# An encoder trunk on one Trainium2 core: a pair of sums, the weight sums, the variance and conv's squares change places

## The chip, the cores and the metric

The kernel runs on one core of a Trainium2 chip. The metric is the time of one launch on the device in microseconds; of several runs the median is taken. TensorE (PE) multiplies, VectorE (DVE) and ScalarE (ACT) do the work element by element, SyncE's queue (SP) issues the transfers of weights.

## The reference

Two layers run over two sequences of 512 and 256 tokens, 768 columns in all. Layer 0 mixes tokens by windowed attention, layer 1 by a gated convolution of width 3. Each layer then has a feed-forward network and a gated embedding.

```python
D_MODEL, D_FF, DEPTH = 1024, 4096, 2
def trunk(x, p, ...):
    for i in range(DEPTH):
        h = rms_norm(x, norm_mix[i])
        x = x + (window_attention if i % 2 == 0 else short_conv)(h, ...)
        h = rms_norm(x, norm_mlp[i])
        x = x + jnp.square(jax.nn.relu(h @ mlp_w_up[i])) @ mlp_w_down[i]
        gate = jax.nn.sigmoid(rms_norm(x, norm_ple[i]) @ ple_w_gate[i])
        x = x + (p[i] @ ple_w_proj[i]) * gate
    return rms_norm(x, final_norm)

def rms_norm(x, g):
    return x * lax.rsqrt(jnp.mean(x * x, axis=-1) + EPS) * g

def short_conv(h, w_in, conv_w, w_out):
    b_gate, c_gate, u = jnp.split(h @ w_in, 3, axis=-1)
    ...   # z = c_gate * u, three taps of z, times b_gate
    return (b_gate * conv) @ w_out
```

## The kernel before

**Layout.** Features lie on the partitions, the 768 tokens on the free axis. x is eight blocks of 128 features by 768 tokens. Most matmuls are 128 by 128 by 384, half the tokens (`H`).

**Precision.** A float32 operand is split into a high part, which ScalarE makes by a copy (`whi`, `zhi`, `vhi`), and a low part, which VectorE makes by a subtraction (`wlo`, `zlo`, `vlo`, line 443). A product takes high by high, high by low and low by high. So a chunk of weights is ready only when VectorE has made its low part.

**Seven products in place of eight.** Large products are done as seven block products over sums of blocks (a scheme of Strassen's kind). Both operands need sums: of the weights `sums32` and `sums14` (lines 405 to 413, two VectorE steps of 128x512 each), of the normalised input `combine(m)` for each m of four. A `combine` pairs blocks m and m+4 of x: two ScalarE copies scaled by the gain (`q`), four VectorE steps 384 wide (`t13` and `t42`, lines 343 to 349), two ScalarE copies for the high parts and two VectorE steps 768 wide for the low parts (`t`, line 359). The first two chunks of a feed-forward's up projection, and the first chunks of conv, are done plainly instead (`up_plain`, `plain_product`, line 1474), because the sums aren't ready yet.

**Norms.** The division by the root mean square is put off: products are made from `xs`, x times the gain, and the scale `r` is applied to the results. `Norm.block` runs for each block of x when it is done: it makes high and low `xs` (line 310 and 311 for the second half of the blocks) and adds the block's squares to `acc` (line 199). The sum of squares over the partitions is a product with ones (`ss`, line 238), its parts `ah` and `al` are split on line 86 and 87. `rstd_steps` then gives five steps, `logs` (variance `v`, line 255, and a logarithm), `root`, `square`, `newton` and `result`.

**Where it happens.** Layer 0's output projection runs over the blocks in the order 0, 4, 1, 5, 2, 6, 3, 7 (`PAIRED`), i counting the places. For each it multiplies (`mm`, line 132), adds to x (`add`, line 1280), runs `n1.block`, then `behind(i)` of `second_inputs`, which loads and splits the second layer's embedding input and its projection (at i = 3) and the first weights. After it come the `pj` products of `ahead`, 48 matmuls, and then the feed-forward: two plain chunks u = 0 and 1, the first seven-product chunk u = 2, an up chunk u = 3, and from there down and up chunks in turn. In `ahead` VectorE makes the low part of the first weights, `acc`'s parts and combined pairs 0 and 1. Layer 1 has conv in the place of attention; its norms and its feed-forward work the same way.

**What sets the order.** ScalarE, TensorE and VectorE each run their instructions in the order in which the code above issues them (`manual_schedule`); no scheduler moves them. So the place of a call in the code is the place in the queue. `pend` is a list of steps that `late()` takes one at a time and issues between the steps of a chunk: in `seven_parts` they are the squares and sums of the chunk before. PSUM's eight banks are shared under the tags A, B and C.

**Names.** In `seven_parts`, `a`, `b`, `c` and `d` are PSUM banks of the products, `y` the chunk's result, `act` its high and low parts. `y L1592` is `y22`, VectorE's read of `a` and of p after the s1 product. The product with w22 uses `vhi` and `vlo`, that with s2 and s3 `zhi` and `zlo`.

## Time and profile before

| | |
|---|---|
| median of three runs | 1646.12 us (1645.8, 1646.12, 1646.88) |
| profiled execution | 1647.11 us, its span 1645.3 us |
| granted TensorE clock | 0.998 |
| busy: TensorE, its weight loads | 99%, 96% of the span |
| busy: VectorE, ScalarE, GpSimd | 84%, 56%, 1% |
| chain that ended last | PE 90%, DVE 5%, DMA 2%, ACT 2%, issue 1% |
| DMA | 144.80 MB, mean 88 GB/s, 27.8% of the 16 engines |

A row of a timeline gives the start in the span and the busy time (both us), the engine, the line, the operation, output<-input, the shape and how many alike were run together; in brackets, how long the engine had been idle before and what it had waited for. A row of the waits gives engine, buffer and line, what released it, the total wait, its count and its longest. PEld is TensorE's weight load, which runs beside the matmul ahead of it.

Where the places lie in the span: layer 0's output projection runs from about 262 to 287 us, the pj products to 295.7, the first plain chunk from 295.7, the second from 313.1, the first seven-product chunk from 329.8. Conv starts at 840.9. Layer 1's feed-forward starts at 1088.3, its first seven-product chunk at 1122.3.

### The profile page before, as it was taken

The page shows a single profiled execution, that of the slowest core. Times are in us where ns is not written, and L with a number is a line of the kernel's source. Part 1 is how long each engine was busy: PE and PEld are TensorE (multiplying, and loading weights), DVE is VectorE, ACT ScalarE, POOL GpSimd, SP SyncE. Part 2 cuts the span into 40 slices and gives each one's busy share as a digit, 9 for nine tenths or more (in the row PEclk, how much of TensorE's full clock was granted, in tenths as well). Part 3 has the DMA queues.
Part 4 walks back from the last instruction along what each step waited for, and adds up shares of the span by engine and source line. Part 5 has one row for each costly group of instructions (what it writes and reads, how often), then busy time and mean ns, then how long its engine had stood idle before and what let it go on. Part 6 is the DMA issues. An engine that isn't in the chain of part 4 may idle for free.

```text
span 1645.3 us, 24138 instructions
## 1 busy us (share of the span) xinstructions
PE 1627.5 (99%) x9371; PEld 1575.4 (96%) x9371; DVE 1389.8 (84%) x2212; ACT 920.7 (56%) x1458; POOL 12.3 (1%) x60
## 2 busy tenths in 40 slices
PE   9999999999999999999999999999999999999998
PEld 7988889999999999999999999999999999999987
DVE  7578987999899989977878888769989989999686
ACT  7378884765555545545654344555545555655465
POOL 0000000000000000000000000000000000000000
PEclk9999999999999999999999999999999999999999
DMA  8745303222221222232311222211222222222332
GB/s 309 193 131 135 107 26 96 93 75 74 68 77 66 76 65 85 70 93 78 116 61 52 77 77 77 78 52 53 76 67 85 67 68 74 78 67 75 118 97 87
DMA packets 47822, 144.80 MB, mean 88 GB/s; under 512 B 6075, under 2 KB 9531, under 8 KB 47708
## 3 DMA queue, kind: packets, MB, share of 16 engines
q1 hardware_dynamic: 47708, 143.27, 27.8%
q8 instruction: 73, 1.20, 0.3%
q14 instruction: 41, 0.34, 0.1%
HBM read 123.85 MB, written 9.96 MB: 81 GB/s over the span
## 4 chain that ended last, share of the span: by engine, by line
PE 90%; DVE 5%; DMA 2%; ACT 2%; issue 1%; SPq 0%; DVEq 0%; POOL 0%; ACTq 0%; POOLq 0%
PE a L464 32%; PE b L464 8%; PE mm L132 8%; PE mm L680 8%; PE d L464 5%; PE c L464 5%; PE p L1474 4%; PE gate L1811 4%; PE B L464 4%; PE C L464 4%; PE gate L132 2%; PE down L1811 2%; PE pt L1129 1%; PE O L1144 1%; PE S L1086 1%
## 5 line engine op out<-in xcount | busy, mean ns | idle before, releaser
L432 ACT ACTIVATE whi<-sum 128x1024 fp32r<-128x1024 f32 x66 | 70.2, 1063 | 253.4 <-PE a L464 251.7
L464 PE MATMUL a<-xs,whi 128*128 128x384 f32 x608 | 118.0, 335 | 1.3 <-DVE y L1592 1.3
L464 PEld LDWEIGHTS a<-xs,whi 128*128 128x128 f32 x608 | 106.4, 188 | 2.3 <-DVE y L1592 2.0
L464 PE MATMUL b<-t,zhi 128*128 128x384 f32 x528 | 106.7, 334 | 0.0
L464 PE MATMUL a<-t,zhi 128*128 128x384 f32 x528 | 106.6, 334 | 0.0
L464 PE MATMUL a<-t,whi 128*128 128x384 f32 x528 | 106.6, 334 | 0.0
L1633 DVE TENSOR_TENSOR x<-x,a 128x384 f32<-128x384 f32 x112 | 62.1, 554 | 51.3 <-PE a L464 51.2
L464 PE MATMUL a<-act,whi 128*128 128x384 f32 x448 | 95.6, 334 | 0.0
L464 PEld LDWEIGHTS a<-t,whi 128*128 128x128 f32 x528 | 92.9, 188 | 0.0
L464 PEld LDWEIGHTS b<-t,zhi 128*128 128x128 f32 x528 | 92.9, 188 | 0.0
L464 PEld LDWEIGHTS a<-t,zhi 128*128 128x128 f32 x528 | 92.9, 188 | 0.0
L432 ACT ACTIVATE zhi<-sum 128x1024 fp32r<-128x1024 f32 x66 | 69.8, 1058 | 38.5 <-DVE sum L408 32.7
L443 DVE TENSOR_TENSOR wlo<-wraw,whi 128x1024 fp32r<-128x1024 f32 x72 | 87.6, 1217 | 0.0
L432 ACT ACTIVATE whi<-wraw 128x1024 fp32r<-128x1024 f32 x72 | 75.7, 1051 | 19.3 <-issue 15.6
L680 PE MATMUL mm<-xs_mix,whi 128*128 128x512 f32 (+1 forms) x320 | 81.4, 341 | 0.0
L443 DVE TENSOR_TENSOR zlo<-sum,zhi 128x1024 fp32r<-128x1024 f32 x66 | 80.3, 1217 | 0.5 <-ACT zhi L432 0.5
L443 DVE TENSOR_TENSOR wlo<-sum,whi 128x1024 fp32r<-128x1024 f32 x66 | 80.4, 1218 | 0.0
L464 PEld LDWEIGHTS a<-act,whi 128*128 128x128 f32 x448 | 79.3, 188 | 0.0
L464 PE MATMUL a<-xs,wlo 128*128 128x384 f32 x304 | 64.9, 334 | 0.0
L464 PE MATMUL b<-t,zlo 128*128 128x384 f32 x264 | 61.1, 335 | 0.7 <-DVE zlo L443 0.7
L464 PE MATMUL a<-t,zlo 128*128 128x384 f32 x264 | 60.9, 334 | 0.0
L464 PE MATMUL a<-t,wlo 128*128 128x384 f32 x264 | 60.9, 334 | 0.0
(391 smaller groups left out, 4480.2 us busy)
## 6 DMA issues: line engine op xcount, KB each, us to landing
wraw<-in_up SPq DMA_DIRECT2D x64, 512.0 KB, 3.4
wraw<-in_down SPq DMA_DIRECT2D x64, 512.0 KB, 3.5
wraw<-in_w_in SPq DMA_DIRECT2D x24, 512.0 KB, 3.4
wraw<-in_gate SPq DMA_DIRECT2D x16, 512.0 KB, 3.5
wraw<-in_w_q SPq DMA_DIRECT2D x8, 512.0 KB, 6.2
wraw<-in_w_out SPq DMA_DIRECT2D x8, 512.0 KB, 3.6
x_in<-in_x SPq DMA_DIRECT2D x8, 384.0 KB, 6.9
pj<-L SPq DMA_DIRECT2D x8, 384.0 KB, 5.7
```

Of the source, the lines that this page charges most:

```text
L132: pe.matmul(t, lhsT=w, rhs=x[:, o:e], start=first and i == 0 and j == 0, stop=last and i == n - 1 and j == 2)
L432: act.activation(hi[:], src, AF.Copy)
L443: dve.tensor_tensor(lo[:], src, hi[:].bitcast(F32), ALU.subtract)
L464: pe.matmul(ps, lhsT=a, rhs=b, start=start and i == 0, stop=i == len(terms) - 1, skip_group_check=True)
L680: pe.matmul(ps.t[:, :n], lhsT=a_, rhs=b_, start=k == 0 and j == 0, stop=k == len(xs) - 1 and j == 2,)
L1086: pe.matmul(S.t[:, :w], lhsT=q, rhs=khh_[g].t[:, kk], start=True, stop=False)
L1129: pe.transpose(pt.t[:, h * P : (h + 1) * P], lg[h // 2].t[:, h % 2, 1 + b * P : 1 + (b + 1) * P], ident[:],)
L1144: pe.matmul(O.t[:], lhsT=vb, rhs=part.t[:], start=b == 0 and i == 0, stop=b == nk - 1 and i == 1)
L1474: pe.matmul(ps[i][o], lhsT=wt[:, c], rhs=xs[f"x{h + 1}{1 + o}"][m][part], start=k == 0 and j == 0, stop=k == KB - 1 and j == 2,)
L1633: dve.tensor_tensor(t[:, o : o + H], t[:, o : o + H], f, op)
L1811: pe.matmul(ps.t[:, o : o + n], lhsT=a_, rhs=b_, start=begin and i == 0 and j == 0, stop=end and i == len(terms) - 1 and j == 2,)
```

## The change

There are four edits. They add and drop no step: each one moves steps in the order in which they are issued.

1. In layer 0's feed-forward, `combine(0)` is issued in the output projection, right behind the third block (i = 2). It takes four places of its own (`apart`). `ahead` now issues pairs 1 and 2 instead of 0 and 1, and the first plain chunk pair 3 alone instead of 2 and 3.
2. In the first plain chunk, `rooted` gives way to `woven`: the variance (`logs`) and the first step of the last pair come ahead of the low part of the next weights (layer 1), and the pair's steps are spread otherwise between the root's steps.
3. In `seven_parts`, the first seven-product chunk of each feed-forward (`soon`) makes the weight sums `sums32` of the next chunk right behind the copy to `c`, ahead of the previous chunk's steps, and no longer behind the copy to `p`.
4. In conv's first plain chunk, the product of the squares with ones, and the variance steps behind it, stand after the first two of the eight blocks of the second product instead of ahead of it; the other six blocks follow.

```diff
 class Norm7:
+            self.apart = self.free if apart is None else list(apart)
 ...
         def combine(self, m):
-            sums = Sums(None, None, [self.free.pop(0) for _ in range(4)], self.xs, m)
+            sums = Sums(None, None, [self.apart.pop(0) for _ in range(4)], self.xs, m)
+    def woven(steps, combined, w):
+        if w:
+            w.high("direct")
+        run(steps, 1)
+        run(combined, 1)
+        if w:
+            w.low("direct")
+        run(combined, 2)
+        run(steps, 1)
+        run(combined, 2)
+        run(steps, 1)
+        run(combined)
+        run(steps)
 def second_inputs(norm, places): def behind(i):
+            elif i == 2:
+                run(norm.combine(0))
 def ahead:
-        c0, c1 = (norm.combine(i) for i in range(2))
+        c0, c1 = (norm.combine(i) for i in (1, 2))
 def seven_parts(w, xs, make, then, first, late, out, soon=False):
         act.activation(c, a, AF.Copy)
+        if more7 and soon:
+            v.sums32()
         late(3 if first else 1)
 ...
         act.activation(p, b, AF.Copy)
-        if more7:
+        if more7 and not soon:
             v.sums32()
 def up_plain (u == 0):
-                v, c0, c1 = w1, *(norm.combine(m) for m in todo)
+                v, *c = w1, *(norm.combine(m) for m in todo)
 ...                                                  # product is set in layer 0
                         v.split("direct")
-                        run(c0, 2)
+                        run(c[-1], 2)
                         norm.table()
                         ss = norm.sum_squares(psum, parts=parts, tag="C")
-                        run(c0)
-                        run(c1, 2)
                     else:
                         parts = norm.acc_parts()
-                        two(c0, c1)
+                        two(*c)
 ...
                             ss = norm.sum_squares(psum, parts=parts, tag="C")
-                            v.split("direct")
-                        rooted(norm.rstd_steps(psum, ss), c1)
+                        woven(norm.rstd_steps(psum, ss), c[-1], None if product else v)
 def up:
-            v = seven_parts(w, xs, make, then, u == PLAIN[l], late, out)
+            v = seven_parts(w, xs, make, then, u == PLAIN[l], late, out, u == PLAIN[l])
 mlp:
-                todo = todo[2:]
+                todo = todo[3:]
 mixer_conv: plain
             products(0, 1)
+            plain_product(ps[0], w, xs, 1, (0, 2), (0, 1))
             ss = norm.sum_squares(psum, parts=sq, tag="C")
 ...
-            for n in range(2, 4):
-                products(0, n)
+            plain_product(ps[0], w, xs, 1, (2, 6), (0, 1))
+            products(0, 3)
             products(1, 0)
 layer 0's output projection:
-    n1 = Norm7(2, "mlp0", xs0, act0[7:11], act0[11])
-    behind, product, w0 = second_inputs(xs0[24:])
+    n1 = Norm7(2, "mlp0", xs0[:12], act0[7:11], act0[11], apart=xs0[12:])
+    behind, product, w0 = second_inputs(n1, xs0[24:])
```

VectorE's instructions in the second half of layer 0's output projection, before the change. `x` behind `xa,mm` is the add of a projected block, `xs` and `x` behind `vec` the low parts of the scaled input, `acc_mlp` the sum of squares, `wlo` the low part of proj's weights:

```order
L1280 TENSOR_TENSOR x<-xa,mm 128x384 x2
L311 SCALAR_TENSOR_TENSOR xs_3313<-x,vec,xs_3312 128x768
L199 TENSOR_TENSOR acc_mlp_3236<-acc_mlp_3236,sq 128x768
L1280 TENSOR_TENSOR x<-xa,mm 128x384 x2
L87 TENSOR_TENSOR wlo<-wraw,whi 128x1024
L306 SCALAR_TENSOR_TENSOR xs_3353<-x,vec,xs_3353 128x384
L306 SCALAR_TENSOR_TENSOR x_3354<-x,vec,x_3354 128x384
```

The same place with the change; `q` are the four 384-wide steps of the pair, `t` its two low parts, one line number is added by the edit:

```order
L1281 TENSOR_TENSOR x<-xa,mm 128x384 x2
L344 TENSOR_TENSOR q<-q 128x384
L312 SCALAR_TENSOR_TENSOR xs_3313<-x,vec,xs_3312 128x768
L199 TENSOR_TENSOR acc_mlp_3236<-acc_mlp_3236,sq 128x768
L345 TENSOR_TENSOR q<-q 128x384
L1281 TENSOR_TENSOR x<-xa,mm 128x384 x2
L349 SCALAR_TENSOR_TENSOR q<-q 128x384
L360 TENSOR_TENSOR t_3369<-q,t_3368 128x768
L307 SCALAR_TENSOR_TENSOR xs_3353<-x,vec,xs_3353 128x384
L307 SCALAR_TENSOR_TENSOR x_3354<-x,vec,x_3354 128x384
L199 TENSOR_TENSOR acc_mlp_3236<-acc_mlp_3236,sq 128x768
L350 SCALAR_TENSOR_TENSOR q<-q 128x384
```

Six steps of the pair now stand between the adds of x (the last, a second `t`, is below the rows shown), and the low part of proj's weights moves behind them.

VectorE in the first seven-product chunk of layer 0's feed-forward, before. `sum` are the weight sums, `act` the parts of the chunk before, `y` behind `y` the sums of that chunk's results, `vlo` the low part for w22:

```order
L443 TENSOR_TENSOR wlo<-sum,whi 128x1024
L389 TENSOR_TENSOR act<-y_3858,act 128x384
L343 TENSOR_TENSOR y_3858<-y_3858 128x384
L344 TENSOR_TENSOR y_3858<-y_3859,y_3858 128x384
L392 TENSOR_TENSOR act<-y_3859,act 128x768
L443 TENSOR_TENSOR vlo<-wraw,vhi 128x512
L348 SCALAR_TENSOR_TENSOR y_3859<-y_3858,y_3859 128x384
L349 SCALAR_TENSOR_TENSOR y_3859<-y_3859 128x384
L407 TENSOR_TENSOR sum<-wraw 128x512
L408 TENSOR_TENSOR sum<-sum,wraw 128x512
```

The same with the change:

```order
L444 TENSOR_TENSOR wlo<-sum,whi 128x1024
L408 TENSOR_TENSOR sum<-wraw 128x512
L409 TENSOR_TENSOR sum<-sum,wraw 128x512
L390 TENSOR_TENSOR act<-y_3858,act 128x384
L344 TENSOR_TENSOR y_3858<-y_3858 128x384
L345 TENSOR_TENSOR y_3858<-y_3859,y_3858 128x384
L393 TENSOR_TENSOR act<-y_3859,act 128x768
L444 TENSOR_TENSOR vlo<-wraw,vhi 128x512
```

The two sums have moved from behind the six steps of the chunk before to ahead of them.

TensorE in conv's first plain chunk, before and then with the change; `p` are the plain products, `ss` the four matmuls with ones:

```order
L1474 MATMUL p_8801<-xs_8769,zlo 128x384
L1474 MATMUL p_8802<-xs_8769,zlo 128x384
L238 MATMUL ss<-ah,ones 128x384
L238 MATMUL ss<-al,ones 128x384
L238 MATMUL ss<-ah,ones 128x384
L238 MATMUL ss<-al,ones 128x384
L1474 MATMUL p_8803<-xs_8242,whi 128x384
```

```order
L1494 MATMUL p_8803<-xs_8313,wlo 128x384
L1494 MATMUL p_8804<-xs_8313,wlo 128x384
L238 MATMUL ss<-ah,ones 128x384
L238 MATMUL ss<-al,ones 128x384
L238 MATMUL ss<-ah,ones 128x384
L238 MATMUL ss<-al,ones 128x384
L1494 MATMUL p_8803<-xs_8400,whi 128x384
```

Twelve matmuls of the second product, p_8803 and p_8804, now stand between the first product and `ss`.

More of the change, by code (lines that the diff above doesn't have):

```diff
@@ L287, in trunk_kernel, with __init__ @@
     class Norm7(Norm):
-        def __init__(self, i, name, places, aside, acc, rstd=None):
+        def __init__(self, i, name, places, aside, acc, rstd=None, apart=None):
             super().__init__(i, name, places, acc, rstd)
             self.free, self.x12 = list(places), list(aside)
+            self.apart = self.free if apart is None else list(apart)
             self.xs = {k: {} for k in (*QS7.values(), "x12")}
@@ L1344, in trunk_kernel, with second_inputs @@
     ET = mybir.EngineType
-    def second_inputs(places):
+    def second_inputs(norm, places):
         part = [], []
@@ L1409, in ahead, with seven_parts @@
         return parts, v
-    def seven_parts(w, xs, make, then, first, late, out):
+    def seven_parts(w, xs, make, then, first, late, out, soon=False):
         w.low("s32")
```

## The prediction

> **What bounds the kernel now.** I read the page first, then the waits of TensorE and of its weight loads (PEld), then the timelines round each wait.

> ```profile
> PE 1627.5 (99%) x9371; PEld 1575.4 (96%) x9371; DVE 1389.8 (84%) x2212; ACT 920.7 (56%) x1458; POOL 12.3 (1%) x60
> ```

> TensorE has work nearly all the time. The number of matmuls does not change, so the change can only move TensorE's waits. The list of waits, matmul rows alone, has three kinds that stand where the diff edits:

> ```profile
> PE a L464 <- DVE y L1592: 1.3, 2, 1.1
> PE b L464 <- DVE zlo L443: 0.7, 2, 0.4
> PE ss L238 <- DVE al L87: 0.2, 1, 0.2
> ```

> That is 2.2 us in five waits. The weight loads tell more. They follow each other without a hole in steady work, and here are the five places, each with the row ahead and the row behind:

> ```profile
> 340.16 1.40 PEld L464 LDWEIGHTS d<-t,vhi 128*128 128x128 f32 x8
> 341.55 0.71 PEld L464 LDWEIGHTS d<-t,vlo 128*128 128x128 f32 x4
> 343.65 1.36 PEld L464 LDWEIGHTS a<-xs,whi 128*128 128x128 f32 x8 [1.40 <-DVE y L1592]
> 345.00 0.71 PEld L464 LDWEIGHTS a<-xs,wlo 128*128 128x128 f32 x4
> ...
> 347.78 0.71 PEld L464 LDWEIGHTS b<-t,zhi 128*128 128x128 f32 x4
> 349.17 0.30 PEld L464 LDWEIGHTS b<-t,zlo 128*128 128x128 f32 x2 [0.69 <-DVE zlo L443]
> 349.46 0.71 PEld L464 LDWEIGHTS b<-t,zhi 128*128 128x128 f32 x4
> ...
> 849.05 0.19 PEld L238 LDWEIGHTS ss<-ah,ones 128*128 128x128 f32 x1
> 849.80 0.19 PEld L238 LDWEIGHTS ss<-al,ones 128*128 128x128 f32 x1 [0.56 <-DVE al L87]
> 850.26 0.19 PEld L1474 LDWEIGHTS p<-xs,whi 128*128 128x128 f32 x1
> ...
> 1133.89 0.71 PEld L464 LDWEIGHTS d<-t,vlo 128*128 128x128 f32 x4
> 1135.15 1.36 PEld L464 LDWEIGHTS a<-xs,whi 128*128 128x128 f32 x8 [0.56 <-DVE y L1592]
> 1136.50 0.71 PEld L464 LDWEIGHTS a<-xs,wlo 128*128 128x128 f32 x4
> 1139.28 0.71 PEld L464 LDWEIGHTS b<-t,zhi 128*128 128x128 f32 x4
> 1140.68 0.30 PEld L464 LDWEIGHTS b<-t,zlo 128*128 128x128 f32 x2 [0.69 <-DVE zlo L443]
> 1140.97 0.19 PEld L464 LDWEIGHTS b<-t,zhi 128*128 128x128 f32 x1
> ```

> The eight loads at 340.16 take 1.39 us to the next group, 0.174 each. From 341.55 to 345.00 twelve loads should take 2.08 us and took 3.45, so the first wait costs 1.37. In the same way 347.78 to 349.46 loses 0.64 (six loads), 849.05 to 850.26 loses 0.51 (four; two rows between are not shown), 1133.89 to 1136.50 loses 0.53 and 1139.28 to 1140.97 loses 0.65. Together **3.70 us**: this is all that the change can gain. The two places at 343 and 1135 are the first seven-product chunk of each feed-forward, the two at 349 and 1140 the first down chunk behind it, 849 is conv.

> [...]

> **The change part by part.**

> *Sums of a pair during the output projection (layer 0).* The first pair's steps leave VectorE's stretch behind 296 us, where VectorE runs without rest up to 343, and enter the projection, where it rests now and then:

> ```profile
> 271.26 1.02 DVE L311 SCALAR_TENSOR_TENSOR xs<-x,vec,xs 128x768 fp32r<-128x768 f32 x1 [1.00 <-ACT xs L310]
> 272.20 0.95 DVE L199 TENSOR_TENSOR acc_mlp<-acc_mlp,sq 128x768 f32<-128x768 f32 x1
> 273.19 1.02 DVE L1280 TENSOR_TENSOR x<-xa,mm 128x384 f32<-128x384 f32 x2
> ...
> 276.35 0.95 DVE L199 TENSOR_TENSOR acc_mlp<-acc_mlp,sq 128x768 f32<-128x768 f32 x1
> 277.22 1.01 DVE L1280 TENSOR_TENSOR x<-xa,mm 128x384 f32<-128x384 f32 x2
> 279.24 1.02 DVE L311 SCALAR_TENSOR_TENSOR xs<-x,vec,xs 128x768 fp32r<-128x768 f32 x1 [1.01 <-ACT xs L310]
> ...
> 285.67 1.02 DVE L1280 TENSOR_TENSOR x<-xa,mm 128x384 f32<-128x384 f32 x2 [0.72 <-PE mm L132]
> ...
> 294.19 1.22 DVE L443 TENSOR_TENSOR zlo<-wraw,zhi 128x1024 fp32r<-128x1024 f32 x1
> ...
> 299.01 0.56 DVE L349 SCALAR_TENSOR_TENSOR q<-q 128x384 f32<-128x384 f32 x1
> 299.48 2.01 DVE L359 TENSOR_TENSOR t<-q,t 128x768 fp32r<-128x768 f32 x2
> ```

> A 384-wide step holds VectorE 0.47 us (299.01 to 299.48), a 768-wide one 0.87 (276.35 to 277.22). The pair is four and two of these: 4 x 0.47 + 2 x 0.87 = 3.62 us. Its first step fits whole into the 1.00 us rest ahead of 271.26. The rest before 273.19 (0.12, since the row at 272.20 is done with its turn at 273.07) and those before 279.24 (1.01) and 285.67 (0.72) take up more. What is left as lateness is 3.62 - 0.47 - 0.12 - 1.01 - 0.72 = 1.30 us. The low part of the first weights, zlo, ended at 295.41 and now ends at about 296.71. TensorE wants it here:

> ```profile
> 296.10 0.19 PEld L1474 LDWEIGHTS p<-x,zlo 128*128 128x128 f32 x1
> ```

> It had 0.69 us to spare; **a new wait of 0.6 us** opens. Bounds: 0 if the rests take up 0.6 us more, and 3.62 - 0.69 = 2.9 if they take up nothing. I take 0.6, since the order puts the steps between the very rows that rested. [...]

> ScalarE's four steps of the pair are no term of their own; the first copy stands ahead of the xs step that waits for x. On VectorE the low part of proj's weights goes behind the steps, some six us later, and with it SP's next fetch into that buffer:

> ```profile
> 263.95 11.78 SPq L92 DMA_DIRECT2D wraw<-in_up  x3
> ```

> The third of these is issued when the buffer comes free, at 275.7; it would be at about 282, some 14 us before the products that come ahead of its use. Nothing.

> *Weight sums ahead of other VectorE work* (`soon`, layers 0 and 1), seen in layer 1:

> ```profile
> 1126.95 0.56 DVE L389 TENSOR_TENSOR act<-y,act 128x384 fp32r<-128x384 f32 x1 [1.67 <-ACT act L379]
> ...
> 1131.15 0.68 DVE L407 TENSOR_TENSOR sum<-wraw 128x512 f32<-128x512 f32 x1
> ...
> 1132.48 0.69 DVE L412 TENSOR_TENSOR sum<-wraw 128x512 f32<-128x512 f32 x1
> ...
> 1134.55 0.55 DVE L1592 TENSOR_TENSOR y<-a,p 128x384 f32<-128x384 f32 x1
> ```

> The two sums cost 1132.48 - 1131.15 = 1.33 us and go into the rest of 1.67 us ahead of act. So y starts 1.33 earlier, at 1133.22, and ends near 1133.8, ahead of the 1134.6 at which TensorE would come (1135.15 - 0.56). zlo at 1139.4 comes up to 1.33 earlier as well, against 0.69 + 0.53 needed once TensorE is earlier: only 0.1 us to spare. Layer 0's VectorE was 0.8 us further behind (1.40 against 0.56), but act there hangs on ScalarE and so on TensorE as in layer 1, once VectorE has caught up by the pair (a pair less behind 296 us, 3.62, against 1.30 of lateness). All four waits go: 1.37 + 0.64 + 0.53 + 0.65 = 3.19.

> *Variance ahead.* In layer 1 it moves into a rest of VectorE:

> ```profile
> 1101.10 1.23 DVE L443 TENSOR_TENSOR zlo<-wraw,zhi 128x1024 fp32r<-128x1024 f32 x1 [2.24 <-ACT zhi L432]
> 1114.12 1.06 ACT L432 ACTIVATE zhi<-sum 128x1024 fp32r<-128x1024 f32 x1 [5.70 <-PE p L1474]
> ```

> What VectorE wins there it loses again at 1114, where ScalarE's zhi waits 5.70 us for a buffer that TensorE holds, and VectorE behind it. I cost it at nothing; if that wait were not there, it would only add to a y that already comes in time.

> *Conv's squares later.*

> ```profile
> 848.79 0.96 DVE L87 TENSOR_TENSOR al<-acc_mix,ah 128x768 fp32r<-128x768 f32 x1 [0.91 <-ACT ah L86]
> ...
> 857.83 1.01 DVE L255 TENSOR_SCALAR v<-ss 128x384 f32<-128x384 f32 x2
> ```

> Twelve matmuls now stand ahead of ss: 12 x 0.174 = 2.08 us, and al was 0.56 late. The wait goes, 0.51 us. The sum reaches VectorE 2.08 us later than at 850.3, five us before v at 857.83. What follows starts from TensorE, so the gain is kept.

> **Sum.** -3.19 - 0.51 + 0.6 = -3.1 us. The profiled execution took 1647.1 us (span 1645.3), and would take 1644.0. The median of the runs is 1.0 lower, 1646.1, so I forecast **1643.0 us**, 0.19% less. About 0.2% (3.3 us) is what a measurement of this kernel can tell from no change; the forecast lies just inside.

> **Rivals.** (1) *No new wait.* The rests take up the last 0.6 us: -3.7, 1642.4. For: four rests are small change that I count only in part. Against: VectorE has no rest from 286 to 296. (2) *The new wait is large*: the steps wait for ScalarE where I let them flow, and no rest is filled: 2.9 - 3.7 = -0.8, 1645.3. (3) *The down chunks' waits stay*, because 0.1 us to spare is too little: 0.64 + 0.65 given back, -1.8, 1644.3. (4) *Slower*: each of the six steps waits for ScalarE as xs does (1.00 us at 271.26), with the adds of x and the weights queued behind on VectorE. Lateness 3.62 + 6 x 1.00 = 9.6, less 0.69, makes a wait of 8.9 at 296.10, net +5.2, 1651.3. It decides from a wait of 3.7 on (no gain) and 7.0 (slower by 0.2%). Against: the order puts other work between the steps. [...]

> **How the numbers follow.** The forecast has 0.60, rivals 1 to 4 have 0.22, 0.08, 0.07 and 0.03. With the new wait between 0 and 1.1 and half a microsecond from run to run, the forecast lies over the bound in a little under half its cases: 0.28. Rival 1 is over it: 0.22. Faster 0.50, slower 0.03, the rest 0.47. The range 1641.9 to 1644.8 holds the forecast and rivals 1 and 3 with that half microsecond, and leaves out 2 and 4.

> **What would show it.** Right: the weight loads of a, b and ss no longer wait at the five places; p's first zlo load waits about 0.6 us for VectorE near 296; the rest ahead of act in layer 1 is about 0.3 us. Wrong: a wait at 296 of over 1.1 us or none; b waiting for zlo behind the first down chunk; ss or v late in conv; a wait that is at no place named here.

## The result and the profile after

The changed kernel took 1643.53 us (median of 18 runs, 1641.31 to 1645.94), the kernel before beside it 1646.86 us (18 runs, 1644.0 to 1650.01). The ratio is 0.9979, with a 95% interval of 0.9973 to 0.9985. That is 3.3 us by the medians, where the forecast said 3.1. The interval spans about 2.5 to 4.4 us, so that close a match owes something to luck. The profiled execution's span is 1641.9 us.

First the list of TensorE's waits of the changed kernel, matmul rows alone (engine, buffer and line, what released it, us in total, times, longest). All of its rows are here, of the list before only those that the prediction quoted:

```profile
PE S L1087 <- DMA q<-ql: 4.8, 3, 2.7
PE warm L779 <- DVE warm L736: 1.8, 1, 1.8
PE mm L132 <- DVE xa L1198: 0.6, 1, 0.6
PE p L1494 <- DVE zlo L444: 0.5, 1, 0.5
PE gate L132 <- DVE wlo L87: 0.3, 1, 0.3
PE vp L1014 <- DVE vv L1032: 0.2, 1, 0.2
PE pt L1130 <- ACT L L1117: 0.2, 1, 0.2
```

The rows of a for y, of b for zlo and of ss for al are gone. p for zlo is new, and so is vp for vv, a row of layer 0's attention, which no edit touches. The weight loads at the new wait and at four of the five old places:

```profile
295.38 0.41 PEld L1494 LDWEIGHTS p<-x,zhi 128*128 128x128 f32 x2
296.60 0.19 PEld L1494 LDWEIGHTS p<-x,zlo 128*128 128x128 f32 x1 [0.80 <-DVE zlo L444]
296.70 0.36 PEld L1494 LDWEIGHTS p<-xs,zhi 128*128 128x128 f32 x2
...
341.98 0.71 PEld L465 LDWEIGHTS d<-t,vlo 128*128 128x128 f32 x4
342.68 1.40 PEld L465 LDWEIGHTS a<-xs,whi 128*128 128x128 f32 x8
...
347.53 0.36 PEld L465 LDWEIGHTS b<-t,zlo 128*128 128x128 f32 x2
...
849.39 0.19 PEld L238 LDWEIGHTS ss<-ah,ones 128*128 128x128 f32 x1
849.56 0.19 PEld L238 LDWEIGHTS ss<-al,ones 128*128 128x128 f32 x1
...
1137.20 0.36 PEld L465 LDWEIGHTS b<-t,zlo 128*128 128x128 f32 x2
```

At 342.68 eight loads now follow 0.70 us behind four others: no hole. At 849.56 al is there when its turn comes. Behind 256 us the hole at 296.60 is the only new one.

**A ledger of the waits.** Each of the twelve traces holds the same 9371 weight loads, so load number n of one trace can be set against load n of another. For each place I take the time between a load ahead of it and one behind it, and subtract the shortest such time in all the twelve profiled executions of this study (the kernels named here are described in the next section). What is left is the time lost there, in us. The last column is the whole stretch from load 1500, at 256 us, to the last load:

```
                  296    343    349    806    850   1135   1140   256 us to the end
                  zlo      y    zlo   gate     ss      y    zlo
before              0   1.36   0.64   0.71   0.51   0.52   0.65   1380.25
changed          0.75      0      0   0.57      0      0      0   1377.14
changed again    0.75      0      0      0      0      0      0   1376.52
no_pair             0   1.05   0.67   0.72      0      0      0   1378.21
no_soon          0.74   0.51   0.67      0      0   0.51   0.67   1378.89
pair_only        0.75   0.52   0.67      0   0.51   0.51   0.67   1379.40
no_conv          0.75      0      0   0.65   0.51      0      0   1377.66
no_woven         0.76      0      0   0.63      0      0      0   1377.20
swap                0      0      0      0      0      0      0   1375.80
swap again          0      0      0   0.71      0      0      0   1376.50
two_pairs        6.05      0      0      0      0      0      0   1382.79
two_pairs_swap   0.37      0      0      0      0      0      0   1377.12
```

The kernels with two pairs lose 0.96 and 0.95 us more at 288 us, at the pj products; no other trace loses time there.

From before to changed the stretch is 1380.25 - 1377.14 = 3.11 us shorter. The columns give -1.36 - 0.64 - 0.51 - 0.52 - 0.65 + 0.75 = -2.93, and -0.14 at the gate, which the change doesn't touch. The stretch from the first load to load 1500 is not edited either, and in the twelve traces it takes 254.1 to 256.3 us. That scatter is as large as the effects, so the verdicts below rest on the ledger, and the times stand beside them. The expectations below put the new wait at 0.83 us; by the ledger it is 0.75.

### The profile page after: what moved, and what is told of

Read it like the earlier page. It is cut to its first block, busy times and chain, and to the rows that moved or that the text cites. A ratio compares the mean times of both kernels' runs of the same rounds, so it can differ in the third digit from the quotient of the medians.

```text
span 1641.9 us, 24136 instructions
## 1 busy us (share of the span) xinstructions
PE 1625.1 (99%) x9371; PEld 1573.5 (96%) x9371; DVE 1389.6 (85%) x2212; ACT 920.6 (56%) x1458; POOL 12.3 (1%) x60
## 4 chain that ended last, share of the span: by engine, by line
PE 92%; DVE 4%; DMA 2%; ACT 1%; issue 1%; SPq 0%; DVEq 0%; ACTq 0%
PE a L465 33%; PE b L465 8%; PE mm L681 7%; PE mm L132 6%; PE p L1494 6%; PE d L465 5%; PE c L465 5%; PE gate L1828 4%; PE B L465 4%; PE C L465 4%; PE gate L132 3%; PE down L1828 2%; PE pt L1130 1%; PE O L1145 1%; PE S L1087 1%; PE S L1088 1%
```

## The experiments

### Undoing the pair, undoing the weight sums, the pair alone

These three ask which edit clears layer 0's first seven-product chunk.

no_pair, the changed kernel without the first edit and without layer 0's part of the second, which hangs on it (the main lines of the edit):

```diff
 behind(i):
-            elif i == 2:
-                run(norm.combine(0))
 ahead:
-        c0, c1 = (norm.combine(i) for i in (1, 2))
+        c0, c1 = (norm.combine(i) for i in range(2))
 ...
-                        woven(norm.rstd_steps(psum, ss), c[-1], None if product else v)
+                        if product:
+                            rooted(norm.rstd_steps(psum, ss), c[-1])
+                        else:
+                            woven(norm.rstd_steps(psum, ss), c[-1], v)
 ...
-                todo = todo[3:]
+                todo = todo[2:]
```

> The changed kernel without the first edit: pairs 0 and 1 are combined behind 291 us again, and the first plain chunk takes pairs 2 and 3; the other three edits stay. My theory: the pair is what lets VectorE catch up in layer 0, and the weight sums alone only put the same work in another order ahead of y. So the new wait at 296 us (0.83 us in the changed kernel's weight loads) goes, and layer 0's wait for y at 343 us comes back nearly whole, 1.1 to 1.37 us, with the 0.64 of the down chunk; layer 1's two waits and conv's stay gone. Against the changed kernel -0.83 + 1.1 to 1.37 + 0.64 = +0.9 to +1.2 us; against the kernel before -2.0 to -2.4 us. Rival: the weight sums alone clear layer 0's two waits, since they take 1.33 us of the 1.40 out of the way; then this kernel is 0.8 us faster than the changed one, -4.2 us against before.

Measured: 1644.62 us, ratio to the kernel before 0.9986 (0.9977 to 0.9995). The ledger has 1.05 at 343, 0.67 at 349 and nothing at 296, so 1.05 + 0.67 - 0.75 = +0.97 against the changed kernel (1378.21 - 1377.14 = 1.07 with the gate's 0.15 in it). That is the theory's +0.9 to +1.2, though the wait at 343 is just under the 1.1 to 1.37 it named; the rival's -0.8 is out.

no_soon, the changed kernel without the third edit:

```diff
-            v = seven_parts(w, xs, make, then, u == PLAIN[l], late, out, u == PLAIN[l])
+            v = seven_parts(w, xs, make, then, u == PLAIN[l], late, out)
```

> The changed kernel without the third edit: the weight sums come behind the copy to p again in both layers. My theory: with the pair moved, layer 0's first seven-product chunk stands as layer 1's did before, so both layers show the waits that layer 1 had: y 0.53 us and zlo in the down chunk 0.65 us in each, 2.35 us in all. The new wait at 296 us stays at 0.8. Against the changed kernel +2.35 us, against the kernel before -1.37 + 0.53 - 0.51 + 0.83 = about -0.5 us. Rival: the pair alone clears layer 0, since it takes 2.3 us out of VectorE's stretch behind 296 us where 1.40 is missing; then only layer 1's two waits come back, +1.2 us against the changed kernel.

Measured: 1647.24 us, ratio 0.9996 (0.9988 to 1.0005). All four waits are back, 0.51 + 0.67 + 0.51 + 0.67 = 2.36, as expected (2.35). So the rival, that the pair alone clears layer 0, is out.

pair_only, the kernel before with the first edit and layer 0's part of the second (the main lines, against the kernel before):

```diff
 behind(i):
+            elif i == 2:
+                run(norm.combine(0))
 ahead:
-        c0, c1 = (norm.combine(i) for i in range(2))
+        c0, c1 = (norm.combine(i) for i in (1, 2))
 ...
+                        if product:
+                            woven(norm.rstd_steps(psum, ss), c[-1], None)
```

> The kernel before with the first edit alone (the last pair's steps in layer 0's first plain chunk in the order of the second edit, which in layer 0 goes with it). My theory: the pair buys only what layer 0's first seven-product chunk was later than layer 1's, 1.37 - 0.53 = 0.84 us, and pays the new wait at 296 us, 0.83: no change against the kernel before, within 0.3 us. Rival, the pair as the edit that carries layer 0: -1.37 - 0.64 + 0.83 = -1.2 us.

Measured: 1646.83 us, ratio 0.9996 (0.9987 to 1.0005). The wait for y at 343 falls from 1.36 to 0.52 and the wait at 296 costs 0.75: no gain, as expected.

So neither edit is worth much in layer 0 without the other. (The pair and layer 0's order of the variance were moved together in these runs; what that order is worth by itself in layer 0 stays open.) VectorE's timeline ahead of act shows why. The kernel before, then the pair alone, then the weight sums without the pair, then the changed kernel:

```profile
335.45 0.56 DVE L389 TENSOR_TENSOR act<-y,act 128x384 fp32r<-128x384 f32 x1 [0.21 <-ACT act L379]
```

```profile
335.94 0.56 DVE L390 TENSOR_TENSOR act<-y,act 128x384 fp32r<-128x384 f32 x1 [1.80 <-ACT act L380]
```

```profile
336.34 0.68 DVE L408 TENSOR_TENSOR sum<-wraw 128x512 f32<-128x512 f32 x1
...
337.67 0.55 DVE L390 TENSOR_TENSOR act<-y,act 128x384 fp32r<-128x384 f32 x1
```

```profile
333.16 0.69 DVE L408 TENSOR_TENSOR sum<-wraw 128x512 f32<-128x512 f32 x1
333.88 0.69 DVE L409 TENSOR_TENSOR sum<-sum,wraw 128x512 f32<-128x512 f32 x1
335.05 0.56 DVE L390 TENSOR_TENSOR act<-y,act 128x384 fp32r<-128x384 f32 x1 [0.48 <-ACT act L380]
...
341.32 0.55 DVE L1609 TENSOR_TENSOR y<-a,p 128x384 f32<-128x384 f32 x1
...
346.18 1.21 DVE L444 TENSOR_TENSOR zlo<-sum,zhi 128x1024 fp32r<-128x1024 f32 x1
```

Before, VectorE rested 0.21 us ahead of act. With the pair gone from its queue it gets there earlier, but act waits for ScalarE, so the time becomes a rest of 1.80 us. The two sums, 1.80 - 0.48 = 1.32 us, can be hidden only in such a rest: without the pair they find about 0.2, and the wait for y falls by no more than 1.36 - 1.05 = 0.31. With both edits the rest of 1.80 takes them in. Then y ends at 341.87, ahead of the load at 342.68, and zlo at 347.39, ahead of the load at 347.53: 0.14 us to spare.

### Undoing conv's move and layer 1's order

no_conv:

```diff
-            plain_product(ps[0], w, xs, 1, (0, 2), (0, 1))
             ss = norm.sum_squares(psum, parts=sq, tag="C")
 ...
-            plain_product(ps[0], w, xs, 1, (2, 6), (0, 1))
-            products(0, 3)
+            for n in range(2, 4):
+                products(0, n)
             products(1, 0)
```

> The changed kernel without the fourth edit: the sum of conv's squares stands ahead of the second product again. My theory: the wait of ss for al comes back and nothing else moves: +0.5 us between the loads ahead of conv and the end, against the changed kernel. Rival: the earlier sum lets the variance and the root come earlier, which conv's later steps use, so that half or more of it is won back by 905 us, where a waits 0.36 us for t: +0.2 or less.

Measured: 1645.13 us, ratio 0.9991 (0.9982 to 1.0). The wait of ss is back with 0.51, and the stretch to the end is 1377.66 against 1377.14, +0.52 (0.08 of it at the gate). Nothing is won back at 902 us, where the twelve traces agree within 0.04.

no_woven:

```diff
-                        woven(norm.rstd_steps(psum, ss), c[-1], None if product else v)
+                        if product:
+                            woven(norm.rstd_steps(psum, ss), c[-1], None)
+                        else:
+                            v.split("direct")
+                            rooted(norm.rstd_steps(psum, ss), c[-1])
```

> The changed kernel with layer 1's part of the second edit undone: the low part of the next weights comes ahead of the variance again, the last pair's steps as in the kernel before. My theory: nothing that TensorE waits for changes, 0 us within 0.1 in the starts of the weight loads. Rival: the variance is what brings r, and by it the first chunks' squares and act, in time; then y's wait in layer 1 comes back in part, up to +0.5 us.

Measured: 1644.52 us, ratio 0.9985 (0.9976 to 0.9993); no wait in the ledger changes but the gate's, by 0.06, and the stretch is 1377.20 against 1377.14. In layer 1 this order is worth nothing.

### Taking the new wait away

swap, the changed kernel with one exchange:

```diff
 second_inputs: behind(i)
             elif i == 7:
-                ws[1].split("second")
+                ws[1].split("direct")
 ahead:
-        w.split("direct")
+        w.split("second")
```

> The changed kernel with one more exchange: the first weights of layer 0's feed-forward are split in the order direct (zhi, zlo), then second (whi, wlo), where it was second, then direct. The plain chunk takes the direct group first, from 295.4 us on, and the second group only half way. zlo moves into the place of wlo, some 3 us earlier on VectorE, between the last add of x and the last low part of xs. My theory: the new wait at 296 us was VectorE being 1.4 us late with zlo and nothing else, so it goes, and nothing takes its place: -0.8 us against the changed kernel, about -4.2 us against the kernel before. Rival: zhi can't be made before TensorE lets its buffer go at about 287.6 us (the last projection's weights lie there), ScalarE gets to it late behind the copies of pj, and VectorE waits for it with the adds and squares queued behind, so that the parts of the squares come late for the sum behind the first product; then no gain, or up to 1 us lost.

Measured: 1642.93 us beside a before of 1647.34, ratio 0.9974 (0.9964 to 0.9985). VectorE's timeline of this kernel:

```profile
294.04 1.22 DVE L444 TENSOR_TENSOR zlo<-wraw,zhi 128x1024 fp32r<-128x1024 f32 x1
...
297.04 1.22 DVE L444 TENSOR_TENSOR wlo<-wraw,whi 128x1024 fp32r<-128x1024 f32 x1
```

zlo stands 3 us ahead of wlo, and no wait takes the place of the one removed. It was run once more:

> The changed kernel with the exchange of the first weights, once more, beside the kernel before on this chip. Theory: no wait for zlo at 296 us, -0.9 us against the changed kernel in the starts of the loads, apart from the gate's wait near 806 us, which goes with the length of a transfer (ScalarE waits about 3 us for it: 0.6 to 0.7; about 2.2: none). In time 4 us less than the kernel before, a ratio of 0.9975 within 0.001. Rival: the first comparison was flattered by the scatter, and the ratio is that of the changed kernel, 0.998 to 0.9985.

Measured: 1642.94 us beside a before of 1646.97, ratio 0.9979 (0.997 to 0.9987). In the ledger swap is 1375.80 without the gate's wait and 1376.50 with it, the changed kernel 1376.52 and 1377.14: 0.6 to 0.7 us less, like against like, where 0.8 and 0.9 were expected. The runs' times alone don't tell the two kernels apart, since the intervals of the ratios overlap; swap's lead over the changed kernel rests on the ledger.

### Doubling the price

two_pairs combines pair 1 in the projection as well:

```diff
             elif i == 2:
                 run(norm.combine(0))
+            elif i == 4:
+                run(norm.combine(1))
 ...
-        c0, c1 = (norm.combine(i) for i in (1, 2))
+        c0, c1 = norm.combine(2), [lambda: None] * 8
```

> The changed kernel with a second pair, pair 1, combined in layer 0's output projection as well, behind the fifth block (i = 4), in place of the stretch behind 296 us. It doubles the suspected price of the first edit. My theory: the rests of VectorE between 269 and 296 us are used up by the first pair (0.4 us of one is left), so the second pair's 3.62 us all end in lateness, and the wait for zlo at 296 grows from 0.83 to between 4.0 and 4.5 us, or the same sum lies in part ahead of it, at the pj products, if proj's weights come late too. Nothing is won back behind it, since the four waits of the seven-product chunks are gone already: +3.2 to +3.7 us against the changed kernel, about the time of the kernel before. Rival: ScalarE's steps of the pair, with the x adds and the xs steps queued behind them, stretch the projection itself by more than the VectorE sum, +5 us or more. [...]

Measured: 1648.49 us, ratio to the kernel before 1.0017 (1.0007 to 1.0026): slower, by 0.2%. The weight loads, and the windows round the wait (columns: us, busy us and instructions of each engine, granted clock, share of the DMA engines, GB/s):

```profile
290.69 0.30 PEld L1397 LDWEIGHTS pj<-p,whi 128*128 128x128 f32 x2 [1.13 <-ACT pjs L1409]
...
301.14 0.29 PEld L1496 LDWEIGHTS p<-x,zlo 128*128 128x128 f32 x1 [3.34 <-DVE zlo L444]
301.31 0.65 PEld L1496 LDWEIGHTS p<-xs,zhi 128*128 128x128 f32 x2
...
307.07 0.45 PEld L1496 LDWEIGHTS p<-xs,zhi 128*128 128x128 f32 x2
307.51 0.19 PEld L1496 LDWEIGHTS p<-xs,zlo 128*128 128x128 f32 x1
```

```profile
297.01:300.43 3.42, 1.11 (x6) 0.68 (x4) 3.42 (x5) 2.16 (x4) 0.00 (x0) 1.00 0.77 285
300.43:303.84 3.41, 2.69 (x8) 2.70 (x9) 3.24 (x6) 2.77 (x4) 0.00 (x0) 0.50 0.58 215
303.84:307.25 3.41, 3.41 (x12) 3.41 (x12) 2.84 (x4) 2.40 (x4) 0.00 (x0) 0.50 0.23 85
307.25:310.67 3.42, 3.42 (x22) 3.42 (x21) 0.65 (x1) 0.00 (x0) 0.00 (x0) 1.00 0.42 152
```

The wait grew to 3.34 us, and TensorE lost 0.96 us more at the pj products, which wait for ScalarE's copies. That much is the theory: 3.34 + 0.96 - 0.75 = 3.55, inside its 3.2 to 3.7. What it did not count is the clock: the loads behind the wait go 0.32 us apart, not 0.174 as in the steady rows of the prediction, because the granted clock is 0.50 from 300.43 to 307.25. The 21 loads from 301.14 to 307.51 take 6.37 us in place of 21 x 0.174 = 3.65, so the clock costs 2.7 us of the ledger's 6.05 at this place.

Against changed again the profiled run lost 1382.79 - 1376.52 = 6.27 us behind 256 us, the median of the runs 1648.49 - 1644.46 = 4.0. The clock did not fall so in each of those runs, which spread from 1646.5 to 1653.17. The mean granted clock of each run is on record: 0.996 in three of the ten, the profiled one among them, 0.997 in three and 0.998 in four. A mean that rounds to 0.998 is 0.9975 or more, and so leaves at most 0.0025 x 2 x 1649 = 8.2 us at one half. In each of the twelve traces the clock is at one half for the last 2.9 us or more, so a stretch of 6.83 us doesn't fit into those four runs. The price of the clock is thus paid in some runs of the same kernel and not in others.

In the profiled run the clock fell to 0.50 at 300.43 us, 2.3 us after the last matmul's end at 298.12, and of the 3.42 us ahead of the fall TensorE was busy for 1.11.

two_pairs_swap, with the exchange of swap added, tests whether the length of the wait did it:

```diff
             elif i == 7:
-                ws[1].split("second")
+                ws[1].split("direct")
 ...
-        w.split("direct")
+        w.split("second")
```

> The kernel with two pairs in the projection, and with it the exchange of the first weights (zlo in the place of wlo). In the kernel with two pairs TensorE waited 3.3 us for zlo at 301 us, and its granted clock was 0.50 for some 6 us behind it. Here zlo would end where wlo ended there, near 298.1, some 0.3 to 0.5 us behind the time at which TensorE asks for it. Theory: the length of the idle window is what lowered the clock, so with a wait of 0.5 the clock stays at 1.00, and both the 2.9 us of waiting and the 2.7 us of slow loads go; the 1.1 us at the pj products stays. Against the changed kernel in the starts of the loads from 284 us to the end: +1.07 - 0.83 + 0.4 = about +0.7 us, where two pairs alone had +6.2. Rival: the clock fell for another reason at that place (a second pair's work on VectorE and ScalarE beside it), so loads behind 300 us are slow again: +3 us or more.

Measured: 1644.59 us, ratio 0.9985 (0.9976 to 0.9993). The wait at 296 is 0.37 us, the clock stays at 1.00 in these windows though the second pair's work is there (so the rival is out), and the stretch from 256 us is 1382.79 - 1377.12 = 5.67 us shorter than that of two_pairs:

```profile
286.00:296.00 10.00, 9.31 (x43) 7.63 (x42) 9.96 (x18) 8.67 (x15) 0.00 (x0) 1.00 0.18 69
296.00:306.00 10.00, 9.90 (x56) 9.47 (x56) 9.25 (x12) 7.30 (x10) 0.00 (x0) 1.00 0.55 191
```

Against changed again, which has no wait at the gate either, it is +0.60 (0.37 here and 0.95 at the pj products, less 0.75), where +0.7 was expected.

### The changed kernel again

> The changed kernel once more, on the chip of the three kernels above, as their measure. In the profiles so far TensorE waits 0.6 to 0.7 us for the low part of a gate weight near 806 us in three kernels (before, changed, without the pair) and not at all in three others (without the weight sums, the pair alone, the exchange). My theory: this is no edit's doing. It goes with a transfer of conv's weights issued near 782 us, which comes 0.8 us later in the first three (ScalarE waits 3.0 to 3.1 us for it against 2.1 to 2.3). So here it may be there or not; where ScalarE's wait for that transfer is about 3 us, the gate's wait is 0.6 to 0.7, where it is about 2.2, there is none. Rival: it belongs to the kernel's order, and the changed kernel shows it again with 0.6 us however long that transfer takes. The other waits as in the first profile: 0.8 us at 296, none at the five old places.

Measured: 1644.46 us, ratio 0.9987 (0.9978 to 0.9996). The wait at 296 is there with 0.75, the gate's is not. ScalarE's row for conv's first weights shows what goes with it, first in the changed kernel's first profile, then in this one:

```profile
786.62 1.06 ACT L433 ACTIVATE zhi<-wraw 128x1024 fp32r<-128x1024 f32 x1 [2.96 <-DMA wraw<-in_w_in]
```

```profile
787.64 1.06 ACT L433 ACTIVATE zhi<-wraw 128x1024 fp32r<-128x1024 f32 x1 [2.13 <-DMA wraw<-in_w_in]
```

In the six traces with ScalarE's wait at 2.96 to 3.10 us the gate loses 0.57 to 0.72 us, in the six with 2.13 to 2.25 it loses nothing. The same program shows both, so the wait goes with the transfer and not with an edit. Why it takes 0.8 us longer in some runs stays open.

## Why the prediction was right, step by step

**The five waits go: right, place by place.** The forecast had 1.37, 0.64, 0.51, 0.53 and 0.65; the ledger has 1.36, 0.64, 0.51, 0.52 and 0.65. Rival 3, that the down chunks' waits stay, is out. Where the prediction had 0.1 us to spare, in layer 1, zlo ends at 1137.06 ahead of its load at 1137.20, and in layer 0 0.14 us is there too:

```profile
1135.85 1.21 DVE L444 TENSOR_TENSOR zlo<-sum,zhi 128x1024 fp32r<-128x1024 f32 x1
```

**The new wait: right in place, 0.75 in place of 0.6.** The term that was mis-sized is the lateness of 1.30 us. VectorE's timeline before, then VectorE's and ScalarE's of the changed kernel:

```profile
266.95 1.02 DVE L1280 TENSOR_TENSOR x<-xa,mm 128x384 f32<-128x384 f32 x2 [1.80 <-PE mm L132]
...
286.60 1.01 DVE L311 SCALAR_TENSOR_TENSOR xs<-x,vec,xs 128x768 fp32r<-128x768 f32 x1
...
292.39 1.02 DVE L311 SCALAR_TENSOR_TENSOR xs<-x,vec,xs 128x768 fp32r<-128x768 f32 x1
...
296.18 0.96 DVE L87 TENSOR_TENSOR al<-acc_mlp,ah 128x768 fp32r<-128x768 f32 x1 [0.76 <-ACT ah L86]
```

```profile
266.63 1.02 DVE L1281 TENSOR_TENSOR x<-xa,mm 128x384 f32<-128x384 f32 x2 [1.90 <-PE mm L132]
...
270.00 0.56 DVE L344 TENSOR_TENSOR q<-q 128x384 f32<-128x384 f32 x1
270.95 1.02 DVE L312 SCALAR_TENSOR_TENSOR xs<-x,vec,xs 128x768 fp32r<-128x768 f32 x1 [0.39 <-ACT xs L311]
...
280.96 1.01 DVE L312 SCALAR_TENSOR_TENSOR xs<-x,vec,xs 128x768 fp32r<-128x768 f32 x1
...
287.66 1.02 DVE L312 SCALAR_TENSOR_TENSOR xs<-x,vec,xs 128x768 fp32r<-128x768 f32 x1
...
293.52 1.02 DVE L312 SCALAR_TENSOR_TENSOR xs<-x,vec,xs 128x768 fp32r<-128x768 f32 x1
...
295.32 1.22 DVE L444 TENSOR_TENSOR zlo<-wraw,zhi 128x1024 fp32r<-128x1024 f32 x1
```

```profile
286.69 0.94 ACT L311 ACTIVATE xs<-x,vec 128x768 fp32r<-128x768 f32 x1 [0.45 <-DVE x L1281]
...
292.54 0.95 ACT L311 ACTIVATE xs<-x,vec 128x768 fp32r<-128x768 f32 x1
```

The first step did go into the rest ahead of xs, of which 0.39 us is left. zlo ends at 296.54. This run is 0.32 us ahead at the start of the projection's row (266.63 against 266.95 before), so the lateness is 296.54 + 0.32 - 295.41 = 1.45 us, and 1.45 - 0.69 = 0.76. Row by row, the same way, it is 280.96 + 0.32 - 279.24 = 2.04 us where the sum of the prediction stands at 3.62 - 0.47 - 0.12 - 1.01 = 2.02; then 287.66 + 0.32 - 286.60 = 1.38, where the last rest of 0.72 should have left 1.30; and 293.52 + 0.32 - 292.39 = 1.45. At both of the later places xs starts 0.03 us after ScalarE has made its high part (287.63 and 293.49), so there VectorE had to wait for ScalarE, which the sum left out. Why ScalarE's part comes that late isn't shown.

The prediction also reads VectorE as without rest from 296 to 343 us. It rested there, 0.76 us at the longest, ahead of al at 296.18. No wait of the forecast hangs on it.

Rival 1, no new wait, is out, and so is rival 2's 2.9. The 1.1 us up to which the prediction lets the new wait go is shown by no run: the six traces with one pair in the projection and zlo in its old place show 0.74 to 0.76.

**The rest ahead of act in layer 1: 0.47 us in place of 0.3,** in the same direction and with no effect on a wait:

```profile
1124.72 0.56 DVE L390 TENSOR_TENSOR act<-y,act 128x384 fp32r<-128x384 f32 x1 [0.47 <-ACT act L380]
```

**Variance ahead at nothing: right** in layer 1, by no_woven; layer 0's part was not run by itself. **Conv's move: right**, 0.51 kept to the end.

**That the pair and the weight sums hold layer 0 together** stood in the prediction only as half a sentence (VectorE has caught up by the pair). The runs made it the main point: without the pair 1.05 + 0.67 us come back in layer 0, without the weight sums 0.51 + 0.67.

**Rival 4, slower,** needed the steps of the pair to wait for ScalarE one by one. They did not. A kernel slower by 0.2% came in another way, by two pairs: in its profiled run a wait of 3.34 us, and behind it 6.83 us at a granted clock of 0.50, as the last section shows.

One correction: the kernel's description says that no scheduler moves the instructions. That holds in the feed-forward and in conv. The output projection is outside of it, and its order is a scheduler's, as the pair's steps between the other rows of the listings show.

## What to carry to other kernels

Where TensorE is busy all the time (99% of the span here), look at the starts of its weight loads: the holes there sum to the most that can be gained, and a ledger of them against load numbers resolves 0.05 us where times scatter by 2 us. A step moved ahead of a wait is free only if there is a rest to take it in; moving other work away first may have to make that rest (here the two sums found 0.21 us of it ahead of act, and 1.80 once the pair had gone). And work put into a stage ahead should not stand in front of the operand that the next stage asks for first: exchanging two low parts was worth 0.6 to 0.7 us, nearly the whole wait that the move had opened.

## What the runs showed of the hardware

In attention the clock fell to 0.50 with a wait of 1.87 us in one trace and stayed at 1.00 with one of 2.71 us in another, so the length of the wait, by which two_pairs_swap was expected to keep its clock, does not tell these two apart. The half-speed stretches inside the twelve traces last 3.41 us, only the one behind zlo's wait in two_pairs 6.83, and by the clock records of two_pairs that one begins 129.71 us after the end of the one in attention (170.72 and 300.43 us), which is 38 steps of 129.71 / 38 = 3.413 us, about the length of such a stretch. So I lay a grid of such steps over each trace, starting from its own changes of the clock, and take TensorE's busy time in each step. First the changed kernel run again, then the changed kernel's first profile, then no_conv, all in attention, which no edit touches:

```profile
165.29:168.71 3.42, 1.55 (x11) 1.33 (x11) 1.35 (x4) 0.00 (x0) 0.00 (x0) 1.00 0.49 116
168.71:172.12 3.41, 3.41 (x11) 3.03 (x10) 2.34 (x10) 2.00 (x7) 0.00 (x0) 0.50 0.02 5
```

```profile
162.69:166.10 3.41, 2.12 (x14) 1.75 (x12) 1.43 (x3) 0.59 (x1) 0.00 (x0) 1.00 0.76 214
166.10:169.52 3.42, 1.99 (x12) 1.89 (x13) 1.05 (x5) 0.63 (x3) 0.00 (x0) 1.00 0.05 16
```

```profile
164.92:168.34 3.42, 1.76 (x12) 1.46 (x11) 1.20 (x5) 0.26 (x1) 0.00 (x0) 1.00 0.28 52
```

The stretch in attention is there in 7 of the 12 traces, and it goes with part of the scatter ahead of 256 us, but not all: from the first load to load 1500, no_woven took 255.63 us without it and swap again 254.21 with it.
